# A hybrid decoder block on one core: the heads stage emitted in another order

## The chip, the core and the metric

The kernel runs on one core of a Trainium2 chip. The core has a matrix engine (TensorE, PE in the rows; its weight loads are PEld), three other compute engines (VectorE = DVE, ScalarE = ACT, GpSimd = POOL) and a queue that issues most of its transfers (SyncE = SP). Each engine works through its own list of instructions in the order in which the program was scheduled, and waits where an instruction's inputs or its output buffer are not ready. The metric is the time of one execution on the device in microseconds (us), the median of several runs.

## The reference

One decoder layer over 512 positions of width 1024, in float32. Cut to what matters here:

```
h = rms_norm(x) * (1 + scale1) + shift1            # the conditioning gives six vectors
xr, gr, q, k, v, gm = split(h @ w_in)              # gm: gates of two branches, 2 x 1024
xr = causal_conv4(xr)
r, i = sigmoid(xr @ w_a + b_a), sigmoid(xr @ w_x + b_x)
a = exp(-8 r softplus(-lam));  u = sqrt(1 - a^2) * (i * xr)
hs[t] = a[t] * hs[t-1] + u[t]                      # the recurrence, an associative scan
y_rnn = hs * gelu(gr)
q, k = rope(rms_norm(q) * gq), rope(rms_norm(k) * gk)     # 8 heads, two maps each, 64 wide
o = (softmax(q1 k1^T) - lam softmax(q2 k2^T)) v           # causal, then a norm per head
merged = sigmoid(gm0) * (y_rnn @ w_proj_rnn) + sigmoid(gm1) * (o @ w_proj_attn)
x = x + gate1 * (merged @ w_out)
x = x + gate2 * (relu(h2 @ w_ff1)^2 @ w_ff2)       # h2: norm and modulation again
```

## The kernel before, in words

Every tile has 128 rows; a feature block is 128 features by 512 positions. Products in full precision are made of three matmuls each (`mm3`, lines 129 to 131): every operand is split into a high part (fp32r) and a low part, and high x high, high x low and low x high are added in one PSUM bank. A weight block comes by a transfer (`load_w`), its high part is a cast on ScalarE (wh, line 122), its low part a subtraction on VectorE (wl, line 123), both with two buffers only and at a raised priority; `project` runs 24 matmuls of 512 columns with it.

The stages in order: norm and modulation; projections of the recurrent branch; the first quarter of q and k (heads 0 and 1); convolution, gates of the recurrence and the first half of v; the heads stage; the attention projections (pa) and the merge; the output product; the MLP.

In the heads stage two streams are put together. `heads()` makes the attention heads one after the other, each in four steps i of 128 queries (`softmax_step`: scores sc on TensorE, mask and maximum in one VectorE instruction on line 587, exponential on ScalarE, the weighted difference of the two maps on VectorE line 596; then `weights_t`: transposes aT, their copy aTs; `value_step`: products po; after step 3 `head_norm`). The output of a head is transposed (yT) and split into yah and yal by `head_out`, two steps into the next head (`OUT_AT = 2`). Its buffers: two PSUM banks for the scores (tag sc), one for all transposes (tag tp), one for po (tag o), and four (tag mm) for all the products of the filler.

`fill()` makes the filler, in the order of the string `PLAN` (line 36): g0 to g7 the gates of the first branch (gate functions on line 685), s0 to s7 the recurrence of block n (`lru_scan`: an exponential, line 461, the scan on line 462; `y_rnn`: line 471, then the split into yh and yl), q1 to q3 a quarter of q and k each (heads 2n and 2n + 1), t1 to t3 their transposes and the copies into the form that the heads read, v1 the second half of v, p0 to p7 the projections of the recurrence (each reads all eight yh and yl), m0 to m7 the gates of the second branch (thg). A group between two slashes is emitted at once; after each part of a head step, `UNITS[head] / STEPS` groups are due.

The emitted order is a priority, not the final order: a scheduler lists each engine's instructions by readiness and priority, and a tile whose buffers are all in use waits until an older one is released. The tags that matter: "y" has 24 buffers (`B_Y`, line 69) for the recurrence's inputs, gel, yh and yl, the heads' yah and yal, and thg; wh and wl have two each.

```
yh = slot("y", B_Y, f"yah{hd}", F32R)                 # head_out, line 643
yl = slot("y", B_Y, f"yal{hd}", F32R)
th1.append(gate(KC + n, slot("y", B_Y, f"thg{KC + n}")))    # fill, letter m
```

Of the kernel before, what the change touches and what calls it, by code (L numbers as in the profile page):

```python
# [32 lines left out]

PLAN = ("g0/s0 s1/g1 g2/g3 s2/s3/q1 s4 g4 t1/s5 g5/s6 q2 s7 v1 g6/t2 p0/g7/p1 p2/p3/q3 p4/p5/p6/t3/"
        "p7/m0/m1 m2/m3/m4/m5/m6 m7")
UNITS = [4.25, 5.25, 6.0, 6.75, 5.75, 5.25, 1.75, 5.5]
STEPS = 14
OUT_AT = 2  # L40
# [13 lines left out]
def build(tc, out, x, xT_in, c, pos, vecs, reps, ada, w_xr, w_xr7, w_qk, w_v, w_gr, w_gm, w_lru,  # L54
# [4 lines left out]
    with ExitStack() as es:  # L59
# [636 lines left out]
        def fill():  # L696

            rot = {}
            for group in PLAN.split("/"):
                for op in group.split():  # L700
# [437 lines left out]
```

## Time and profile before

| | us |
|---|---|
| median of 3 runs | 877.34 (877.32 to 877.82) |
| the profiled execution | 876.41 |
| its span, first to last instruction | 874.6 |
| TensorE busy (share of the span) | 861.0 (98%) |
| VectorE busy | 651.5 (74%) |
| ScalarE busy | 449.2 (51%) |

The heads stage lies between about 165 and 455 us of the span. A busy matrix engine means only that a matmul is in flight: a matmul of 512 columns is shown for 0.39 us, though the next one starts 0.23 us after it. Rows of views call tiles by the names in the program with the numbers left out (sc, aT, po, yT, gm, pr). Each window row gives the busy time of each engine in that stretch, and the granted clock of TensorE.

### The profile page before, as it was taken

The page shows a single profiled execution, that of the slowest core. Times are in us where ns is not written, and L with a number is a line of the kernel's source. Part 1 is how long each engine was busy: PE and PEld are TensorE (multiplying, and loading weights), DVE is VectorE, ACT ScalarE, POOL GpSimd, SP SyncE. Part 2 cuts the span into 40 slices and gives each one's busy share as a digit, 9 for nine tenths or more (in the row PEclk, how much of TensorE's full clock was granted, in tenths as well). Part 3 has the DMA queues.
Part 4 walks back from the last instruction along what each step waited for, and adds up shares of the span by engine and source line. Part 5 has one row for each costly group of instructions (what it writes and reads, how often), then busy time and mean ns, then how long its engine had stood idle before and what let it go on. Part 6 is the DMA issues. An engine that isn't in the chain of part 4 may idle for free.

```text
span 874.6 us, 11292 instructions
## 1 busy us (share of the span) xinstructions
PE 861.0 (98%) x4012; PEld 705.5 (81%) x4012; DVE 651.5 (74%) x1251; ACT 449.2 (51%) x748; POOL 15.1 (2%) x50
## 2 busy tenths in 40 slices
PE   6999999999999999999999999999999999999998
PEld 3888887877878888888888888888888888888887
DVE  6997995599859855786758556858766885876397
ACT  6673547985536543535623343747545544554461
POOL 1000000000000000000000000000000000002110
PEclk9999999999999999999999999999999999999999
DMA  8979425412255372238336332822641344139572
GB/s 315 370 250 319 152 97 134 136 68 73 87 131 169 99 191 76 93 87 227 110 126 210 132 121 75 273 87 72 193 148 70 128 161 169 49 126 235 120 122 96
DMA packets 64572, 128.92 MB, mean 147 GB/s; under 512 B 6146, under 2 KB 30850, under 8 KB 64516
## 3 DMA queue, kind: packets, MB, share of 16 engines
q1 hardware_dynamic: 59236, 122.97, 43.3%
q0 software_dynamic: 5280, 5.24, 3.9%
q8 instruction: 31, 0.51, 0.2%
q14 instruction: 25, 0.20, 0.1%
HBM read 113.51 MB, written 2.10 MB: 132 GB/s over the span
## 4 chain that ended last, share of the span: by engine, by line
PE 86%; DVE 10%; DMA 1%; issue 1%; ACT 1%; SPq 1%; ACTq 0%; DVEq 0%
PE f L131 6%; PE f L129 6%; PE f L130 6%; PE X L131 3%; PE X L130 3%; PE X L129 3%; PE gm L129 3%; PE gm L130 3%; PE gm L131 3%; DVE wl L123 2%; PE sc L582 2%; PE qk L131 2%; PE qk L129 2%; PE qk L130 2%; PE xr L129 2%; PE pr L129 2%
## 5 line engine op out<-in xcount | busy, mean ns | idle before, releaser
L122 ACT CAST wh<-w 128x1024 fp32r<-128x1024 f32 (+1 forms) x113 | 118.0, 1044 | 214.5 <-issue 48.1
L123 DVE TENSOR_TENSOR wl<-w,wh 128x1024 fp32r<-128x1024 f32 (+1 forms) x113 | 137.0, 1213 | 68.1 <-ACT wh L122 64.5
L131 PE MATMUL f<-h2h,wl 128*128 128x512 f32 x240 | 93.5, 390 | 0.4 <-DVE wl L123 0.4
L130 PE MATMUL f<-h2l,wh 128*128 128x512 f32 x240 | 93.2, 389 | 0.0
L129 PE MATMUL f<-h2h,wh 128*128 128x512 f32 x240 | 92.9, 390 | 0.0
L131 PEld LDWEIGHTS f<-h2h,wl 128*128 128x128 f32 x240 | 45.0, 188 | 10.1 <-DVE wl L123 0.8
L130 PEld LDWEIGHTS f<-h2l,wh 128*128 128x128 f32 x240 | 45.1, 188 | 9.4
L129 PEld LDWEIGHTS f<-h2h,wh 128*128 128x128 f32 x240 | 45.0, 188 | 9.3
L130 PE MATMUL gm<-hl,wh 128*128 128x512 f32 x128 | 51.0, 398 | 0.0
L129 PE MATMUL qk<-wh,hh 128*128 128x512 f32 x128 | 50.7, 396 | 0.0
L129 PE MATMUL gm<-hh,wh 128*128 128x512 f32 x128 | 50.5, 394 | 0.0
L131 PE MATMUL gm<-hh,wl 128*128 128x512 f32 x128 | 50.5, 394 | 0.0
L131 PE MATMUL qk<-wh,hl 128*128 128x512 f32 x128 | 50.4, 394 | 0.0
L130 PE MATMUL qk<-wl,hh 128*128 128x512 f32 x128 | 50.4, 394 | 0.0
L941 DVE TENSOR_TENSOR p_1l<-b,p_1h 128x1024 fp32r<-128x1024 f32 x24 | 29.4, 1223 | 26.3 <-ACT p_1h L940 26.1
L589 ACT ACTIVATE e<-e,nm 128x128 f32<-128x128 f32 (+3 forms) x64 | 35.7, 559 | 24.4 <-DVE nm L587 24.4
L940 ACT CAST p_1h<-b 128x1024 fp32r<-128x1024 f32 x24 | 25.2, 1051 | 31.0 <-PE f L130 22.9
L941 DVE TENSOR_TENSOR p_0l<-b,p_0h 128x1024 fp32r<-128x1024 f32 x24 | 29.3, 1223 | 15.0 <-ACT p_0h L940 13.8
L587 DVE CUSTOM_DVE_ANT_0 e<-sc,mask 128x128 f32<-128x128 f32 (+3 forms) x64 | 30.3, 484 | 9.9 <-PE sc L582 9.9
L940 ACT CAST p_0h<-b 128x1024 fp32r<-128x1024 f32 x24 | 25.3, 1055 | 24.2 <-PE X L131 12.4
L188 DVE CUSTOM_DVE_ANT_0 ada<-ada,cb,bada 128x1024 f32<-128x1024 f32 x16 | 20.5, 1283 | 14.3 <-DMA ada<-in_ada 14.1
L984 DVE TENSOR_TENSOR b<-b,b 128x1024 f32<-128x1024 f32 x24 | 29.1, 1220 | 0.1
(444 smaller groups left out, 2216.9 us busy)
## 6 DMA issues: line engine op xcount, KB each, us to landing
ada<-in_ada SPq DMA_DIRECT2D x64, 256.0 KB, 5.8
w<-in_w_ff SPq DMA_DIRECT2D x32, 512.0 KB, 3.2
b<-in_w_ff SPq DMA_DIRECT2D x30, 512.0 KB, 3.4
w<-in_w_qk SPq DMA_DIRECT2D x16, 512.0 KB, 3.2
w<-in_w_gm SPq DMA_DIRECT2D x16, 512.0 KB, 3.7
ada<-in_ada SPq DMA_DIRECT2D x16, 512.0 KB, 3.3
b_t<-in_w_ff POOLq DMA_DIRECT2D x10, 512.0 KB, 6.5
w<-in_w_gr SPq DMA_DIRECT2D x8, 512.0 KB, 4.0
```

The costliest lines, as they stand in the source:

```text
L122: i_w = nc.scalar.copy(wh[:, :n], w[:, :n])
L123: nc.vector.tensor_tensor(wl[:, :n], w[:, :n], f32(wh)[:, :n], op=ALU.subtract)
L129: nc.tensor.matmul(ps, lh, rh, start=first, stop=False, skip_group_check=more)
L130: nc.tensor.matmul(ps, lh, rl, start=False, stop=False, skip_group_check=more)
L131: nc.tensor.matmul(ps, ll, rh, start=False, stop=last, skip_group_check=more)
L188: nc.vector.tensor_tensor_reduce(w, w, cb, 1.0, bada[:, col:col + 1], op0=ALU.mult, op1=ALU.add, accum_out=mod[:, col:col + 1])
L582: nc.tensor.matmul(ps[m][:, :nn], q[m][:, qc], k[m][r][:, :nn], start=r == 0, stop=r == 1)
L587: nc.vector.tensor_tensor_reduce(e[:, :n], ps[m][:, :n], mask[:, S - n:], 1.0, 1e30, op0=ALU.add, op1=ALU.min, accum_out=nm)
L589: nc.scalar.activation(e[:, :n], e[:, :n], AF.Exp, bias=nm, scale=-1.0, accum_out=sums[:, m:m + 1])
L940: nc.scalar.copy(v4(wh), v)
L941: nc.vector.tensor_tensor(v4(wl), v, f32(v4(wh)), op=ALU.subtract)
L984: nc.vector.tensor_tensor(d, d, s_, op=ALU.add)
```

## The change

Only the string that orders the filler is another one. The recurrences s1 to s7 are spread over more groups, g4 stands ahead of the second quarter and g6 ahead of the third, and m0 ahead of p0; the number of groups grows by one.

```
-PLAN = ("g0/s0 s1/g1 g2/g3 s2/s3/q1 s4 g4 t1/s5 g5/s6 q2 s7 v1 g6/t2 p0/g7/p1 p2/p3/q3 p4/p5/p6/t3/"
-        "p7/m0/m1 m2/m3/m4/m5/m6 m7")
+PLAN = ("g0/s0/g1 g2/s1 g3/g4/q1 t1/s2 g5/s3/g6 s4 q2 s5 v1/s6 t2/g7 s7/m0/p0 p1/p2/q3 p3/p4/p5/t3/"
+        "p6/p7/m1 m2/m3/m4/m5/m6 m7")
```

Three places of the resulting order follow. The number behind a tile's name counts the program's tiles, so a tile has another one after the change.

TensorE before, in the last quarter of q and k (qk_0 to qk_3: its four PSUM banks), 12 rows after the transposes of head 3's output (yT); aT_1_3535 are the transposes of step 1 of head 4:

```order
L129 MATMUL qk_1_3541<-wh_3546,hh_195 128x512
L130 MATMUL qk_1_3541<-wl_3547,hh_195 128x512
L131 MATMUL qk_1_3541<-wh_3546,hl_199 128x512
L129 MATMUL qk_1_3541<-wh_3546,hh_238 128x512
L130 MATMUL qk_1_3541<-wl_3547,hh_238 128x512
L131 MATMUL qk_1_3541<-wh_3546,hl_242 128x512
L604 MATMUL aT_1_3535<-ident,e_1_0_3459 128x128 x2
L129 MATMUL qk_2_3542<-wh_3546,hh_195 128x512
```

TensorE after, at the same transposes (aT_1_3504 now); pr_4272 is the eighth projection of the recurrence (p7), and yh_1831, yh_1959 and yh_2512 are blocks 0, 1 and 2:

```order
L131 MATMUL pr_4272<-yh_1831,wl_4269 128x512
L129 MATMUL pr_4272<-yh_1959,wh_4268 128x512
L130 MATMUL pr_4272<-yl_1961,wh_4268 128x512
L131 MATMUL pr_4272<-yh_1959,wl_4269 128x512
L129 MATMUL pr_4272<-yh_2512,wh_4268 128x512
L130 MATMUL pr_4272<-yl_2514,wh_4268 128x512
L604 MATMUL aT_1_3504<-ident,e_1_0_3396 128x128 x2
L131 MATMUL pr_4272<-yh_2512,wl_4269 128x512
L129 MATMUL pr_4272<-yh_2577,wh_4268 128x512
L130 MATMUL pr_4272<-yl_2579,wh_4268 128x512
L615 MATMUL po_3387<-vs_0_3159,aTs_1_3507 128x128
```

Step 1's transposes of head 4 have moved from the first unit of the last quarter into the last projection of the recurrence: 220 filler rows now stand between them and head 3's yT.

TensorE before, around step 2 of head 6 (sc_2_0 and sc_2_1 the scores of its two maps, aT_0 and po_4145 the transposes and products of step 0, gm_4424 the gate product m2):

```order
L129 MATMUL gm_4424<-hh_346,wh_4420 128x512
L130 MATMUL gm_4424<-hl_350,wh_4420 128x512
L131 MATMUL gm_4424<-hh_346,wl_4421 128x512
L582 MATMUL sc_2_0_4203<-kh_2_0_4038,qs_0_0_4023 128x384
L604 MATMUL aT_0_4197<-ident,e_0_0_4134 128x128
L582 MATMUL sc_2_0_4203<-kl_2_0_4041,qs_0_0_4023 128x384
L582 MATMUL sc_2_1_4204<-kh_2_1_4044,qs_0_1_4026 128x384
L582 MATMUL sc_2_1_4204<-kl_2_1_4047,qs_0_1_4026 128x384
L615 MATMUL po_4145<-vs_0_3133,aTs_0_4199 128x128
L129 MATMUL gm_4424<-hh_398,wh_4420 128x512
L130 MATMUL gm_4424<-hl_402,wh_4420 128x512
L131 MATMUL gm_4424<-hh_398,wl_4421 128x512
```

TensorE after, at the same step (po_4146 its products, yT_4222 the transposes of head 5's output, gm_4588 the gate product m5):

```order
L582 MATMUL sc_2_0_4204<-kh_2_0_4078,qs_0_0_4063 128x384
L582 MATMUL sc_2_0_4204<-kl_2_0_4081,qs_0_0_4063 128x384
L604 MATMUL aT_0_4198<-ident,e_0_0_4135 128x128
L582 MATMUL sc_2_1_4205<-kh_2_1_4084,qs_0_1_4066 128x384
L582 MATMUL sc_2_1_4205<-kl_2_1_4087,qs_0_1_4066 128x384
L615 MATMUL po_4146<-vs_0_3159,aTs_0_4200 128x128
L642 MATMUL yT_4222<-ident,o_4019 128x128 x4
L582 MATMUL sc_3_0_4239<-kh_2_0_4078,qs_0_0_4063 128x512
L582 MATMUL sc_3_0_4239<-kl_2_0_4081,qs_0_0_4063 128x512
L582 MATMUL sc_3_1_4240<-kh_2_1_4084,qs_0_1_4066 128x512
L582 MATMUL sc_3_1_4240<-kl_2_1_4087,qs_0_1_4066 128x512
L129 MATMUL gm_4588<-hh_195,wh_4584 128x512
```

The gate rows that stood between the scores of steps 1, 2 and 3 are gone from there: they ran ahead of them (gm_4530) or come behind (gm_4588).

VectorE before, at the start of head 6 (e_0_0 and e_0_1: mask and maximum of the two maps of step 0; ql_3: the low part of the last transposed quarter, wl_4459: the weight split of m3):

```order
L123 TENSOR_TENSOR wl_4421<-w_4418,wh_4420 128x1024
L587 ISA e_0_0_4134,nm_0_0_4133<-sc_0_0_4127,mask 128x128
L587 ISA nm_0_0_4133 128x1
L143 TENSOR_TENSOR ql_3_4072<-qT_3_4065,qh_3_4070 128x512
L587 ISA e_0_1_4138,nm_0_1_4137<-sc_0_1_4128,mask 128x128
L587 ISA nm_0_1_4137 128x1
L123 TENSOR_TENSOR wl_4459<-w_4456,wh_4458 128x1024
```

VectorE after, at the same start (wl_4585 and wl_4632: the weight splits of m5 and m6):

```order
L123 TENSOR_TENSOR wl_4585<-w_4582,wh_4584 128x1024
L587 ISA e_0_0_4135,nm_0_0_4134<-sc_0_0_4128,mask 128x128
L587 ISA nm_0_0_4134 128x1
L143 TENSOR_TENSOR ql_1_4097<-qT_1_4090,qh_1_4095 128x512
L123 TENSOR_TENSOR wl_4632<-w_4629,wh_4631 128x1024
L587 ISA e_0_1_4139,nm_0_1_4138<-sc_0_1_4129,mask 128x128
L587 ISA nm_0_1_4138 128x1
L593 RECIPROCAL rr_4126<-sm_0_4127 128x2
```

The split wl_4632 has moved in between the two maps of step 0; its cast reuses the buffer that the product gm_4530 reads.

## Rows read from the trace of the kernel before

**Rows 1.** The page: engine totals, and slices of TensorE's busy share and clock.

```profile
PE 861.0 (98%) x4012; PEld 705.5 (81%) x4012; DVE 651.5 (74%) x1251; ACT 449.2 (51%) x748; POOL 15.1 (2%) x50
...
PE   6999999999999999999999999999999999999998
...
PEclk9999999999999999999999999999999999999999
```

**Rows 2.** Windows: stretch, its length, busy us of each engine, clock, transfers.

```profile
178.00:218.00 40.00, 38.15 (x194) 30.58 (x194) 39.86 (x98) 26.86 (x64) 0.00 (x0) 1.00 0.19 66
...
190.00:200.00 10.00, 8.90 (x53) 7.10 (x52) 9.91 (x25) 6.77 (x19) 0.00 (x0) 1.00 0.21 76
...
240.00:250.00 10.00, 9.26 (x43) 7.08 (x42) 8.83 (x22) 2.59 (x3) 0.00 (x0) 1.00 0.27 96
...
380.00:447.00 67.00, 66.96 (x356) 54.64 (x355) 47.60 (x149) 34.65 (x92) 0.00 (x0) 1.00 0.52 153
...
419.00:437.00 18.00, 17.96 (x101) 14.59 (x101) 13.94 (x49) 10.99 (x32) 0.00 (x0) 1.00 0.25 88
```

**Rows 3.** Waits, heads stage: who waited for whom, total us, times, longest.

```profile
PE aT L604 <- DVE e L596: 1.5, 4, 0.7
PE qT L547 <- DVE raw L535: 0.7, 1, 0.7
...
ACT wh L122 <- PE gm L130: 15.0, 10, 3.9
```

**Rows 4.** The tile yT from 355 to 395 us: durations (ns), first and last start.

```profile
L642 PE MATMUL yT<-ident,o x4: 270/272/273, 366.4 to 366.8; 128*128 128x128 f32 x4
L644 ACT ACTIVATE yah<-yT,sg x1: 678/678/678, 379.6 to 379.6; 128x512 fp32r<-128x512 f32 x1
L646 DVE SCALAR_TENSOR_TENSOR yal<-yT,sg,yah x1: 743/743/743, 380.7 to 380.7; 128x512 fp32r<-128x512 f32 x1
```

**Rows 5.** The tile thg on ScalarE, 395 to 450 us.

```profile
L685 ACT ACTIVATE thg<-gm x8: 589/592/631, 411.4 to 447.9; 128x512 f32<-128x512 f32 x8
```

**Rows 6.** Timeline from 418 to 428 us: start, duration, engine, line, tiles, idle before.

```profile
418.83 0.29 DVE L587 CUSTOM_DVE_ANT_0 e<-sc,mask 128x128 f32<-128x128 f32 x1
...
419.84 0.28 PE L582 MATMUL sc<-kh,qs 128*128 128x256 f32 x1
419.93 0.17 DVE L593 RECIPROCAL rr<-sm 128x2 f32<-128x2 f32 x1 [0.80 <-ACT e L589]
419.95 0.28 PE L582 MATMUL sc<-kl,qs 128*128 128x256 f32 x1
...
421.55 0.34 PE L582 MATMUL sc<-kh,qs 128*128 128x384 f32 x1
...
421.72 0.34 PE L582 MATMUL sc<-kl,qs 128*128 128x384 f32 x1
...
424.44 0.55 DVE L587 CUSTOM_DVE_ANT_0 e<-sc,mask 128x384 f32<-128x384 f32 x1
...
425.87 1.05 ACT L122 CAST wh<-w 128x1024 fp32r<-128x1024 f32 x1
...
426.13 0.60 PE L642 MATMUL yT<-ident,o 128*128 128x128 f32 x4
...
426.48 0.48 PE L582 MATMUL sc<-kl,qs 128*128 128x512 f32 x1
...
426.80 0.39 PE L582 MATMUL sc<-kh,qs 128*128 128x512 f32 x1
...
426.95 1.23 DVE L123 TENSOR_TENSOR wl<-w,wh 128x1024 fp32r<-128x1024 f32 x1
427.03 0.40 PE L582 MATMUL sc<-kl,qs 128*128 128x512 f32 x1
```

**Rows 7.** Groups by line, VectorE, 165 to 455 us: the scans and their neighbours.

```profile
L462 DVE TENSOR_TENSOR_SCAN xc<-r,xc 128x512 f32<-128x512 f32 x8 | 9.7, 1210 | 0.0
```

## The prediction

> **What bounds the kernel now.** I read the page first: TensorE is busy for 98% of the span, at a clock of 1.00 in every slice (2.4 GHz), so a changed order can only win or lose time in which TensorE stands [rows 1]. Then the windows of the heads stage. From 178 to 218 us TensorE is busy 38.15 of 40 us and VectorE 39.86: here VectorE's queue decides, and TensorE loses 1.85 us. From 380 to 447 us, the last heads, TensorE is busy 66.96 of 67 us and VectorE 47.60: nothing is lost there, because a matmul of the filler stands ready behind every step of a head [rows 2]. A third place loses 0.74 us (240 to 250). The waits by name agree: transposes of weights that wait for VectorE's weighted sum (1.5 us), and one wait of the second quarter's transposes (0.7 us) [rows 3]. So at most 2.6 us are to be won in this stage, while the end of it has 19 us of idle VectorE time and no TensorE time to spare.
>
> Two more views show what holds the heads. The four transposes that end head 4 ran from 366.4 us, but their copies on ScalarE and VectorE only at 379.6 and 380.7 [rows 4]. In between the last recurrence projections ran. The copies go into buffers of tag "y", 24 of them; the eight recurrence results take 16 until the last projection reads them, and the outputs of heads 0 to 3 take the other 8. The next transposes of this head need the same single PSUM buffer, so the heads stood for 13 us, and TensorE lived on filler. And the first second-branch gate (thg) left its PSUM bank only at 411.4 us, though four banks are all that the filler products have [rows 5].
>
> **The change, part by part.** No instruction is added but a few splits of merged waits; the work is the same, in another order.
>
> *The hold comes a head earlier.* The first second-branch gate (m0) now stands before the first projection, so one "y" buffer more is taken: 16 + 1 + 6 = 23 when head 3 ends, one is left, and head 3's low part finds none. By the order on TensorE the held transposes (aT of step 1, head 4) come after 8 rows of the eighth projection, 220 filler rows after the transposes of head 3; before, the hold (head 5) was 60 rows long. A row starts 0.23 us after the one before it (426.80 and 427.03) [rows 6], so 60 rows are 13.7 us, which is what rows 4 show, and the new hold is about 50 us. While it lasts nothing is lost: TensorE has its 220 rows. What is lost comes behind it: the rest of head 4 and heads 5, 6 and 7 must run beside 16 + 168 rows, where before the rest of head 5 and heads 6 and 7 had 12 + 192 rows. The tail gets one head more and one gate product less.
>
> *Term A, a wait in front of head 6.* The four PSUM banks are full (gates 1 to 4) when gate 4's product ends, since the gate function of gate 1 now stands on ScalarE behind an exponential of head 6, step 2. So the next filler can't start. In VectorE's queue a weight split (wl_4632) stands ahead of the mask-and-max of the second map of step 0, and it waits for a cast that waits for the last row of gate 4's product, whose buffer it takes; such casts waited 15 us in all for gate products before, where filler covered it [rows 3]. From that last row's start: 0.39 us for the row, 1.08 from cast to split, 1.14 for the split to the next start (1.23 less the 0.08 by which a next one starts early), 0.29 for the mask-and-max: 2.90 us until TensorE may write the bank again [rows 6]. It has in the meantime the row itself (0.23), four 256-wide score rows (0.12 each) and four transposes (0.35 to the next start at 426.48, so 0.09 each; I take 0.44 with the hand-over): 1.1 us. A = 2.9 - 1.1 = **1.8 us**. Bounds: 0 if the bank is freed by another path, 2.0 with a delay of 0.1 at each hand-over.
>
> *Term B, the chain of head 6.* Behind it TensorE's queue has only rows of this head up to the last score of step 3, and each waits for VectorE. The same chain in head 7 before, from the mask-and-max of step 0 (418.83) to the end of that of step 2 (424.44 + 0.55), took 6.2 us, with a wait of 0.80 us for an exponential in it [rows 6]; TensorE filled it with gate rows. There it also held eleven tiny instructions of the norm, which are elsewhere now (up to 1.8 us, some in gaps), and now holds one 512-wide split (0.69). I take 5.3 us, less the first 0.29: 5.0. TensorE's work in it: scores of 0.24 + 0.35 + 0.35 + 0.46 (256-wide 0.12 a row, 384-wide 0.17, 512-wide 0.23), a transpose and a value row of 0.11, and four transposes of 0.44, together 2.06. B = 5.0 - 2.1 = **2.9 us**; bounds 2.3 (one more overlap) and 3.8 (the whole measured 6.2).
>
> *Term C, the rest of the tail.* One head more costs VectorE no more than 11.4 us (13.94 busy from 419 to 437, which holds all of head 7, less one split of 1.23 and one 1.29), so it goes from 47.6 to at most 57.9 of 67 us with one split of 1.14 gone [rows 2]. That still fits, so throughput asks for nothing; but the steps of heads 4, 5 and 7 now have 2 to 10 rows between them. Nearest rows: this tail before lost 0.04, and the stretch where VectorE was full lost 1.85 in 40 us, which over 67 us is 3.1. I take **2.0**, bounds 0 and 4.
>
> *Term D, the front.* In VectorE's order the scans are hardly later: a scan is 1.21 us [rows 7], and the eighth now comes before step 2 of head 1 is summed, where it came after step 3. What changes is that one gate product more (24 rows, 5.5 us of TensorE) stands before the second quarter, with its split (1.14), and three of the splits of finished recurrences (0.60 each) slip behind the stretch: VectorE 39.86 - 0.7 = 39.2 us against TensorE's 38.15 + 5.5 = 43.6. The queue is no longer full, but two scans in a row now stand ahead of a sum that a transpose waits for. I take **-1.0**, bounds 0 and -1.85. The 0.74 us at 245 stays: its chain and the 92 rows that cover it are the same; its bounds are 0 and -0.74.
>
> The SP queue issues the same transfers; the weight loads of gates 4 to 6 pass the copies of the last quarter, and a load has two products' time (11 us) to land, so nothing is charged.
>
> The sum: 1.8 + 2.9 + 2.0 - 1.0 = +5.7 us. The profiled execution took 876.41 us (span 874.6), so it would take 882.1; the median shown is 0.93 above that execution, which gives **883.0 us**.
>
> One rule of the Trainium skill speaks against this. "Perfetto Trace Analysis", Optimization Strategy, says that where the most-contended engine changes over time, interleaving the regimes can help. Rows 2 show such regimes (VectorE 39.86 of 40 us in one, 47.60 of 67 in the other), and by the rule alone the sum would be term D with the 0.74, at most -2.6 us: the first rival below.
>
> **The rivals.**
> 1. *The front's waits go and the tail keeps its cover* (faster). The scans spread out, TensorE gets the 1.85 us and some of the 0.74 back, and A and B vanish because the gate functions free their banks in time. For it: TensorE was full in the tail (0.04 lost), and VectorE has 19 us there. Against: 57.9 of 67 us and the order itself, which puts no filler row between the scores of head 6. About -2: 875.3 us.
> 2. *The front's gain pays for a small tail* (no change): only B's lower end counts and D is full: 2.3 - 1.85 = +0.5: 877.8 us.
> 3. *The order does not do what it says*: the scans stay where they were, D is 0, and the tail costs what I sum: +6.7, 884.0 us. It lies inside my own range.
> 4. *VectorE becomes the bound of the whole tail* (worse): waits for exponentials of 0.80 us at two or three places of each step add up to C = 4 to 6 on top of A and B at their upper bounds (5.8): +10, 887.4 us. It decides if VectorE's busy share from the release to the last head's norm is above 9 tenths.
> 5. *The clock falls.* Before, a window with 1.10 us of idle TensorE kept 1.00 [rows 2]; no row shows a longer gap after the start. If the half-filled 7 us of A and B brought the granted clock to its lower level (1.2 GHz), one gate product behind it would take twice its 5.5 us: +11.2, 888.5 us. The Trainium skill, "TensorE: Matmul & The Clock Gate", HAM oscillation, states that idle gaps can throttle the array again; the rows so far (1.00 in every window) don't bear that out here.
>
> **How the numbers follow.** My forecast (+3 to +9, with rival 3) has 0.74, rival 4 0.08, rival 5 0.03, rival 2 0.07, rival 1 0.08. About 0.2% (1.75 us) is what a measurement can tell from no change: slower 0.86 (mine, 4, 5 and 0.01 of rival 2), same 0.06, faster 0.08. With all low bounds (A 0, B 2.3, C 0, D -1.85 and -0.74) the sum is -0.3, with all high ones +9.8, and rivals 4 and 5 go on to +11; I leave out a tenth at either end: 878.6 to 888.0 us.
>
> **What would show it.** Right: the copies of head 3's output 45 us or more after its transposes; TensorE full while they wait; then, in the last 70 us before the attention projections, a stretch of some 7 us with about 4.7 us of idle TensorE, in which the waits are named after mask-and-max and the sums; the first second-branch gate but one leaving its bank only there; and 178 to 223 us with about 1 us less idle time. Wrong: gate rows running between the scores of head 6; or the loss lying in front of 230 us; or no wait longer than 1 us in the tail.

## The result, and the profile after

The changed kernel takes 884.24 us (median of 5 runs, 883.65 to 884.72), the kernel before 877.34 us in the same comparison (876.54 to 877.91): a ratio of 1.0077 with a 95% interval of 1.0063 to 1.0092. That is slower, as forecast (883.0 us, range 878.6 to 888.0). The profiled execution took 883.81 us with a span of 882.0, 7.4 us more than before.

The page of the changed kernel, its engine totals and the granted clock:

```profile
PE 864.7 (98%) x4012; PEld 707.4 (80%) x4012; DVE 652.4 (74%) x1251; ACT 449.6 (51%) x748; POOL 15.1 (2%) x50
...
PEclk9999999999999999999899999999999999999999
```

TensorE runs the same 4012 instructions, but is busy for 3.7 us longer than in [rows 1] and idle for 3.7 us longer (17.3 against 13.6 us). So half of the loss is idle time, and the other half is rows that are shown for longer; one slice of the clock row has an 8 instead of a 9. The windows of the changed kernel say where (columns as in [rows 2]):

```profile
178.00:218.00 40.00, 37.83 (x191) 30.79 (x190) 39.44 (x93) 25.35 (x60) 0.00 (x0) 1.00 0.19 66
...
250.00:290.00 40.00, 39.27 (x205) 32.14 (x205) 30.20 (x86) 21.99 (x54) 0.00 (x0) 1.00 0.59 158
...
410.00:420.00 10.00, 8.61 (x43) 6.68 (x41) 5.18 (x11) 3.61 (x6) 0.00 (x0) 1.00 0.85 217
420.00:430.00 10.00, 8.91 (x35) 6.67 (x36) 6.90 (x26) 6.35 (x18) 0.00 (x0) 0.66 0.79 213
```

The front did not get better: 2.17 us idle from 178 to 218 us against 1.85 in [rows 2], and the 0.73 us of the second quarter's chain are there again, 5 us later. The tail lost 2.48 us of idle time in 20 us, and a third of the clock in the second half of them; VectorE was busy for only 12 of those 20 us.

Idle time does not see rows that are merely slower or further apart. So this table measures losses otherwise: from the start of each matmul to the start of the next one, less the median of that difference for its width (0.227 us for 512 columns, 0.177 for 384, 0.119 for 256, 0.109 for 128, from the kernel before). The sum over a stretch is what TensorE lost there, in us:

| stretch, us | before | changed | e1 | e2 | e3 | e5 | e9 |
|---|---|---|---|---|---|---|---|
| 178 to 230 | 3.7 | 3.6 | 3.6 | 3.7 | 3.5 | 3.5 | 3.8 |
| 230 to 375 | 2.9 | 2.6 | 2.9 | 2.9 | 2.8 | 2.7 | 3.1 |
| 375 to 410 | 0.9 | 1.9 | 1.1 | 1.2 | 1.2 | 1.9 | 1.1 |
| 410 to 432 | 0.9 | 6.8 | 0.8 | 8.7 | 1.1 | 0.7 | 0.9 |
| 432 to 470 | 0.3 | 1.4 | 0.7 | 3.0 | 1.2 | 6.1 | 0.3 |

Changed less before, before rounding, gives -0.1, -0.3, +1.0, +6.0 and +1.1: 7.6 us. Ahead of 178 us the changed kernel lost 0.4 us less, which leaves 7.3 of the 7.4 us.

Now the tile yT of the changed kernel from 300 to 470 us, which answers to [rows 4]:

```profile
L644 ACT ACTIVATE yah<-yT,sg x5: 670/688/690, 329.3 to 460.1; 128x512 fp32r<-128x512 f32 x5
L646 DVE SCALAR_TENSOR_TENSOR yal<-yT,sg,yah x5: 745/750/751, 378.7 to 460.8; 128x512 fp32r<-128x512 f32 x5
```

The first of the five is head 3's output. Its high part was copied at 329.3, its low part 49.4 us later: the one buffer of tag y that was left went to the high part, and the low part waited until the last recurrence projection gave buffers back. Before, the hold was 13 us and a head later. While the low part waited, TensorE was full, with 222 rows:

```profile
329.00:379.00 50.00, 50.00 (x222) 41.16 (x220) 27.70 (x49) 15.87 (x21) 0.00 (x0) 1.00 0.30 100
```

ScalarE's copies of outputs (L644) and second-branch gate functions (L685), changed kernel (start, duration, idle before):

```profile
329.34 0.67 ACT L644 ACTIVATE yah<-yT,sg 128x512 fp32r<-128x512 f32 x1
...
424.97 0.69 ACT L644 ACTIVATE yah<-yT,sg 128x512 fp32r<-128x512 f32 x1 [1.74 <-PE yT L642]
...
426.15 0.58 ACT L685 ACTIVATE thg<-gm 128x512 f32<-128x512 f32 x1
...
427.23 0.59 ACT L685 ACTIVATE thg<-gm 128x512 f32<-128x512 f32 x1
...
428.46 0.60 ACT L685 ACTIVATE thg<-gm 128x512 f32<-128x512 f32 x1
```

Between 329 and 426 us no gate function of the second branch runs; those of m1, m2 and m3 then come one after the other, the first 1.2 us behind the copy of head 5's output. Their products had ended at 396.0, 405.2 and 411.1 us, that of m4 at 417.5; until then m1 to m4 fill all four PSUM banks. TensorE in the same place:

```profile
418.26 0.36 PE L582 MATMUL sc<-kl,qs 128*128 128x256 f32 x1
420.11 0.39 PE L582 MATMUL sc<-kh,qs 128*128 128x256 f32 x1 [1.49 <-DVE nm L587]
420.34 0.28 PE L582 MATMUL sc<-kl,qs 128*128 128x256 f32 x1
421.44 0.69 PE L582 MATMUL sc<-kh,qs 128*128 128x384 f32 x1 [0.82 <-DVE nm L587]
421.93 0.52 PE L582 MATMUL sc<-kl,qs 128*128 128x384 f32 x1
...
425.58 0.63 PE L582 MATMUL sc<-kh,qs 128*128 128x512 f32 x1
426.01 0.63 PE L582 MATMUL sc<-kl,qs 128*128 128x512 f32 x1
426.79 0.79 PE L129 MATMUL gm<-hh,wh 128*128 128x512 f32 x1 [0.15 <-ACT thg L685]
```

Two waits for mask-and-max, and then slower rows: they are shown for 0.52 us with 384 columns and 0.63 with 512, where [rows 6] have 0.34 and 0.40, and two of 512 start 0.43 us apart (425.58 and 426.01) instead of 0.23. The first gate row after them waits for the first gate function. VectorE shows what the first wait is:

```profile
418.62 1.23 DVE L123 TENSOR_TENSOR wl<-w,wh 128x1024 fp32r<-128x1024 f32 x1 [0.83 <-PE sc L582]
419.77 0.28 DVE L587 CUSTOM_DVE_ANT_0 e<-sc,mask 128x128 f32<-128x128 f32 x1
```

That is the weight split which now stands between the two maps of step 0. The view names another releaser, but it starts right behind the cast that it reads (417.56 to 418.59 us). And the clock, in windows of 2 us of the changed kernel:

```profile
418.00:420.00 2.00, 0.62 (x5) 0.42 (x4) 1.38 (x3) 1.13 (x2) 0.00 (x0) 1.00 0.64 137
420.00:422.00 2.00, 1.06 (x4) 0.80 (x4) 1.40 (x8) 1.08 (x4) 0.00 (x0) 0.72 0.71 152
422.00:424.00 2.00, 2.00 (x8) 1.53 (x7) 1.59 (x7) 0.62 (x3) 0.00 (x0) 0.50 0.40 89
424.00:426.00 2.00, 2.00 (x8) 1.72 (x7) 1.34 (x6) 1.03 (x2) 0.00 (x0) 0.50 0.96 207
426.00:428.00 2.00, 1.85 (x7) 0.95 (x6) 1.04 (x4) 1.81 (x6) 0.00 (x0) 0.57 0.90 237
```

### The profile page after: what moved, and what is told of

Read it like the earlier page. It is cut to its first block, busy times and chain, and to the rows that moved or that the text cites. A ratio compares the mean times of both kernels' runs of the same rounds, so it can differ in the third digit from the quotient of the medians.

```text
span 882.0 us, 11295 instructions
## 1 busy us (share of the span) xinstructions
PE 864.7 (98%) x4012; PEld 707.4 (80%) x4012; DVE 652.4 (74%) x1251; ACT 449.6 (51%) x748; POOL 15.1 (2%) x50
## 4 chain that ended last, share of the span: by engine, by line
PE 89%; DVE 7%; ACT 1%; issue 1%; DMA 1%; SPq 0%; ACTq 0%
PE f L131 6%; PE f L130 6%; PE f L129 6%; PE X L130 3%; PE X L131 3%; PE X L129 3%; PE gm L129 3%; PE gm L130 3%; PE gm L131 3%; PE qk L131 3%; PE qk L130 3%; PE qk L129 3%; PE sc L582 2%; PE po L615 2%; PE xr L129 2%; PE v L129 2%
## 5 line engine op out<-in xcount | busy, mean ns | idle before, releaser
L129 PEld LDWEIGHTS gm<-hh,wh 128*128 128x128 f32 x128 | 24.2, 189 | 5.0 <-ACT thg L685 0.9
```

The lines of the kernel that those rows point to most:

```text
L129: nc.tensor.matmul(ps, lh, rh, start=first, stop=False, skip_group_check=more)
```

## The experiments

Twelve kernels ran, each against the kernel before on the same chip in five rounds (its medians there were 876.8 to 877.1 us). Five settle the cause, two the clock, five the front. e1 stands for the label e1_m0_behind, and so on.

**Is it m0's place?** Back behind p7 in the changed order:

```
-g7 s7/m0/p0 p1/p2/q3 p3/p4/p5/t3/p6/p7/m1 m2/
+g7 s7/p0 p1/p2/q3 p3/p4/p5/t3/p6/p7/m0/m1 m2/
```

> The changed order with one letter moved back: m0 behind p7 instead of ahead of p0. Theory 1 (the buffer that m0's gate takes starts the hold a head earlier, and all of the loss lies in the tail behind it): head 4 runs on as before, the hold falls on head 5, the stretch around head 6 loses under 1.5 us instead of 6.8, and the time is 876.5 to 878.0 us (+0.0 +-0.1% against the kernel before). Theory 2 (the loss comes from the other moves, the scans and the gates ahead of the second and third quarter): m0's place does not matter, 883 to 885 us.

Measured: 877.3 us, ratio 1.0005 (0.9996 to 1.0013). And m0 moved ahead of p0 in the order before (the group of t2 and p0 is split for it, so the string has one group more, as the changed one has):

```
-g6/t2 p0/g7/  ...  p7/m0/m1 m2/
+g6/t2/m0/p0/g7/  ...  p7/m1 m2/
```

> The order before with one letter moved: m0 ahead of p0 instead of behind p7. Theory 1: this alone makes the hold of some 50 us on head 4 and the idle time and the lower clock in head 6; 883 to 885 us (+0.7 +-0.15%). Theory 2: 877 to 878 us.

Measured: 887.78 us, ratio 1.0125 (1.0109 to 1.0140). The same window of both, e1 first and then e2:

```profile
420.00:430.00 10.00, 9.84 (x53) 8.02 (x52) 8.24 (x35) 7.17 (x24) 0.00 (x0) 1.00 0.16 54
```

```profile
420.00:430.00 10.00, 8.93 (x29) 6.48 (x29) 6.03 (x24) 5.24 (x15) 0.00 (x0) 0.53 0.76 175
```

One letter makes all of the loss, whichever order it stands in; the scans and the other gates make none, nor does the number of groups, which e1 leaves as the change has it. e2 is 2.8 us above the expected upper end: its last head waits too (3.0 us from 432 to 470).

**Its place, or its buffer?** The changed order, with m0's output elsewhere:

```
-slot("y", B_Y, f"thg{KC + n}")
+slot(*(("y", B_Y) if n else ("v", B_V)), f"thg{KC + n}")
```

> The changed order word for word, but the output of m0's gate goes into a buffer of the value tiles (tag v, free when head 3 is done) instead of tag y. Theory 1: 16 + 8 outputs fit again, the hold moves back to head 5, 877 to 879 us, with a first gate function of the second branch that still comes behind head 5's output. Theory 2, and also the rival that it is m0's place in the row of products and not its buffer: 883 to 885 us.

Measured: 878.24 us, ratio 1.0014 (1.0006 to 1.0023). The next one leaves m0 in tag y and gives the outputs of heads 3 and 4 the four value buffers, so that no head waits:

```
+where = ("v", B_V) if hd in (3, 4) else ("y", B_Y)
-yh = slot("y", B_Y, f"yah{hd}", F32R)            # yal alike
+yh = slot(*where, f"yah{hd}", F32R)
```

> The changed order word for word; the outputs of heads 3 and 4 go into the four value buffers that are free after head 3, so that no head waits for tag y (m0 stays ahead of p0 and in tag y). If the hold and nothing else makes the loss: no copy of an output waits longer than 3 us for a buffer, the tail loses under 1.5 us, 876.5 to 878.5 us. If the hold is only half of it (m0 used up ahead of time is missing as filler at the end): 879 to 882 us, with the loss behind 440 us.

Measured: 877.33 us, ratio 1.0002 (0.9994 to 1.0011). So it is the buffer. With the order of the instructions' source unchanged, one or four buffers more take back 6 to 7 us, and m0 run early is not missed as filler at the end.

**Is it the four banks?** The gate functions of m1 to m4 in the value buffers, the hold left as it is:

```
-slot("y", B_Y, f"thg{KC + n}")
+slot(*(("v", B_V) if 1 <= n <= 4 else ("y", B_Y)), f"thg{KC + n}")
```

> The changed order word for word; the outputs of the gates m1 to m4 go into the four value buffers that are free after head 3 instead of tag y. The hold on head 4 stays as it is (50 us). Theory 1a (tag y hands out its buffers in the program's order, so the gate functions of m1 to m4 wait for head 5's output to take its own, and the four PSUM banks they sit in starve TensorE of filler): the gate functions run 1 to 3 us behind their products, gate rows stand between the scores of head 6, the stretch from the release to the end of head 6 loses under 2 us instead of 6.8, 878.5 to 880.5 us. Theory 1b (the squeezed heads are bound by VectorE's chain whatever the banks do): TensorE still waits 2 us or more for mask-and-max in head 6, 882 to 885 us.

Measured: 882.54 us, ratio 1.0064 (1.0051 to 1.0077). The time lies in the range of 1b, while head 6 does what 1a expected. ScalarE in e5:

```profile
395.79 0.69 ACT L644 ACTIVATE yah<-yT,sg 128x512 fp32r<-128x512 f32 x1 [1.14 <-PE yT L642]
...
397.31 0.60 ACT L685 ACTIVATE thg<-gm 128x512 f32<-128x512 f32 x1
...
407.94 0.58 ACT L685 ACTIVATE thg<-gm 128x512 f32<-128x512 f32 x1
...
412.26 0.59 ACT L685 ACTIVATE thg<-gm 128x512 f32<-128x512 f32 x1
```

The gate functions no longer wait for head 5's output (424.9 us): they run 0.8 to 2.3 us behind their products, against 17 to 30 in the changed kernel. Head 6 loses nothing (0.7 us from 410 to 432). That much of 1a is right: what they waited for is their turn in tag y. In the five kernels where they share it with the heads' outputs (before, changed, e1, e2, e3), the first of those left at that point starts 0.6 to 1.9 us behind the copy of head 5's output, whenever that comes, from 411 to 427 us. But the gate rows that cover head 6 are then missing behind head 7. TensorE in e5:

```profile
459.20 0.63 PE L642 MATMUL yT<-ident,o 128*128 128x128 f32 x4 [1.26 <-DVE o L635]
460.61 1.21 PE L129 MATMUL pa<-yah,wh 128*128 128x512 f32 x2 [0.78 <-ACT yah L644]
```

The stretch from 432 to 470 us lost 6.1 us instead of 1.4. The banks decide where the tail starves, not whether: three and a half heads are left for too little filler.

**What does the lower clock cost?** Useless matmuls into the two gaps of head 6, kept there by order (`after`); their products go into the bank of head 6's value products:

```
+for _ in range(DUMMY[i, m, r]):
+    d_ = nc.tensor.matmul(pre[0], ident, ct..., start=True, stop=True)
+    after(d_, mms[-1])
```

> The changed order with nine useless matmuls of 512 columns in the two gaps of head 6 (six in front of the second map's scores of step 1, three in front of those of step 2; they write a bank that is overwritten). The waits for mask-and-max stay; TensorE is only busy in them. Theory C (the two gaps, 1.5 and 0.8 us, bring the clock down, and the lower clock is some 3 us of the loss): the granted clock stays 1.00 from 418 to 430 us and the time falls to 880 to 882 us. Rival (the clock falls for another reason, or its rows lie beside waits that stay anyway): no change, 883.5 to 885 us.

Measured: 890.39 us, ratio 1.0153 (1.0139 to 1.0167). This run says nothing on the clock: a plain float32 product of 512 columns shows as two rows, 0.43 us from start to start, so nine of them took 7.7 us and outlasted the gaps, and the second three also overwrote a value product (that part of the output is lost) and were waited for. The next kernel uses fp32r operands, and both sets come before any value product:

```
-nc.tensor.matmul(pre[0], ident, ct..., start=True, stop=True)
+nc.tensor.matmul(pre[0], h[0][0][:, :P], h[0][0], start=True, stop=True)
```

> The changed order, every instruction in its place, with nine useless matmuls of 0.23 us in the two gaps of head 6 (six behind the second map's scores of step 0, three behind those of step 1; they write a bank that is overwritten). The fillers of e6_gap_filled took 0.86 us each, so they outlasted the gaps; these do not. Theory C (the two gaps bring the clock down, and the lower clock is some 3 us of the loss): the granted clock stays 1.00 from 418 to 430 us, the stretch from 410 to 432 us loses 3 to 4.5 us instead of 6.8 besides the 2.1 us of useless rows that lie in waits, 880 to 882 us. Rival (the lower clock costs nothing on the path, since head 6 waits for VectorE anyway): 883.5 to 885 us, with waits for mask-and-max longer by what the rows are shorter.

Measured: 883.2 us, ratio 1.0071 (1.0058 to 1.0083), between the two expected ranges. Two windows of e10 that answer to the third and fourth of the 2 us rows above:

```profile
422.00:424.00 2.00, 1.72 (x10) 1.26 (x10) 1.58 (x9) 1.11 (x3) 0.00 (x0) 1.00 0.64 138
424.00:426.00 2.00, 1.86 (x8) 0.87 (x8) 1.32 (x5) 2.00 (x7) 0.00 (x0) 1.00 0.96 206
```

The clock stays up when the gaps are filled, so the gaps brought it down. But faster rows only wait longer: idle time now stands where slow rows stood. The stretch from 410 to 432 us lost 3.6 us and spent 2.0 on the useless rows, 5.6 together, against 6.8. That makes 1.2 us for the clock in the profiles, not 3. The intervals of the two ratios overlap, so the times alone do not show it. One reason lies at the end of the program: the last matmul of e10 starts 2.0 us earlier than that of the changed kernel (876.60 against 878.56 us; 0.4 of it was won ahead of 178 us), but from there to the end of the span e10 takes 4.9 us and the changed kernel 3.4. Why its end is longer stays open.

**Why did the front win nothing?** In the next kernels each recurrence's first VectorE step stands behind the last weighted sum ahead of it in the program. In e7 that is all that changes from the kernel before:

```
+if last_sum:
+    after(i_, last_sum[-1])
```

> The order before, but each recurrence's first VectorE step may not start before the last weighted sum that stands ahead of it in the program, so that the scans stand where the order's string has them: 3, 1, 1, 3 and so on per step instead of up to 7 ahead of a step. Theory D (the 1.85 us of idle TensorE from 178 to 218 us come from scans that VectorE runs ahead of sums): 1 to 1.9 us won, 875.0 to 876.5 us, and VectorE no longer 99% busy there. Rival (VectorE's work in this stretch is the same whatever its order, and the waits only change places): 876.5 to 878.5 us.

Measured: 877.47 us, ratio 1.0005 (0.9996 to 1.0014). The same in e8, on top of e1:

> The changed order with m0 back behind p7 and with the scans pinned to their places in the string, which are spread out to heads 1 to 3. Theory D: the front's waits go (1.85 us and more), the tail is as before: 874.5 to 876.5 us, faster than both kernels. Rival: the waits change places, 876.5 to 879 us.

Measured: 883.06 us, ratio 1.0074 (1.0061 to 1.0087). Windows of e8, the front and the stretch behind it:

```profile
178.00:218.00 40.00, 40.00 (x203) 33.50 (x202) 29.48 (x78) 24.47 (x59) 0.00 (x0) 1.00 0.23 79
...
262.00:340.00 78.00, 73.84 (x362) 58.51 (x361) 70.45 (x189) 41.66 (x100) 0.00 (x0) 0.98 0.47 132
```

Theory D is right about the front: with the scans really spread out, VectorE falls to 29.48 us and TensorE does not wait at all there. By starts, 178 to 230 us lost 0.6 instead of 3.7 us. But now six scans run from 268 to 318 us, beside the norm of the third quarter and in front of the projections that need them, and 230 to 375 us lost 11.5, so the time is above both expected ranges. Two orders between the extremes (e11: s2, s3 ahead of q1; e13: s4 to s7 behind q1):

```
-g4/q1 t1/s2 g5/s3/g6 s4 q2 s5 v1/s6 t2/g7 s7/
+s2/g4/s3 q1 s4 t1/g5/s5 g6/s6 q2 s7 v1/t2/g7/          # e11
+s2/g4/s3 q1 s4 s5 s6 s7 t1/g5/g6/q2 v1/t2/g7/          # e13
```

> The changed order with m0 back behind p7 and the scans pinned, but s2 to s7 each put a group or two earlier than in e8_m0_behind_scans_pinned (s2 and s3 before the second quarter, s7 before the second half of v), so that the last one ends before 290 us. Theory D (VectorE's full queue costs the front its 1.85 us, and in e8 only the projections that waited for the last yh lost 8 us): the front loses 1 to 2 us instead of 3.6, the projections do not wait, 874.8 to 876.5 us. Rival (each scan that is moved costs as much beside the later heads): 876.5 to 878.5 us.

Measured: 877.77 us, ratio 1.0007 (0.9998 to 1.0016).

> As e11_scans_spread (m0 behind p7, scans pinned), but the last three recurrences stand behind the second quarter's products (s5 to s7 between q1 and t1) instead of beside heads 2 and 3: in e11 VectorE was busy for 12 of 24 us from 214 to 226 and from 256 to 268 us, and for 24 of 24 from 268 to 286 and 292 to 298 us. Theory D (what counts is that VectorE is full nowhere while a head runs): the front keeps its 2.5 us, the stretch from 262 to 375 us loses under 2 us instead of 4.9, 874.5 to 876.0 us, ratio under 0.9985. Rival (the three recurrences now delay the norm of the second quarter, for which TensorE waits at 245 us): 876.5 to 878.5 us.

Measured: 879.05 us, ratio 1.0027 (1.0018 to 1.0036), above both expected ranges. In the traces both win 2.5 us in the front (1.2 lost instead of 3.7) and give them back: e11 loses 4.9 us from 262 to 375 (before: 1.6), e13 loses 3.8 from 230 to 262 (before: 1.3), most of it in one wait for the norm of the second quarter:

```profile
251.80 0.30 PE L549 MATMUL qT<-ident,raw 128*128 128x128 f32 x1 [2.67 <-DVE raw L537]
```

The profiled execution of e13 was the fastest of its eleven (877.10 us), so the trace does not show all of its loss: in six others the mean granted clock was 0.998 instead of 1.000, and these took 878.75 to 880.50 us against 877.10 to 879.05. No trace shows where the clock fell in them.

The rival holds in all four: between 178 and 375 us, moving scans moved the waits, and in e8 and e13 made them dearer. The last kernel takes work away from VectorE instead, on the kernel before:

```
-nc.vector.tensor_tensor(hs, hs, g, op=ALU.mult)
+nc.gpsimd.tensor_tensor(hs, hs, g, op=ALU.mult)
```

> The kernel before with the eight products of scan and gelu (0.68 us each on VectorE) on GpSimd, which stands idle in this stretch. If VectorE's busy share of 99% from 178 to 218 us is what makes TensorE wait there, 5.5 us less on VectorE win 0.5 to 1.8 us: 875.2 to 876.6 us. Rival (GpSimd is so slow that the splits behind it come late, or it takes time from VectorE): 877 to 880 us.

Measured: 886.5 us, ratio 1.0106 (1.0093 to 1.0119), far above both expected ranges. The product's row in e12:

```profile
L471 POOL TENSOR_TENSOR xc<-xc,gel x8: 1262/1632/2117, 181.5 to 215.3; 128x512 f32<-128x512 f32 x8
```

1.63 us instead of 0.68, in a chain that TensorE waits for: 178 to 230 us lost 13.5 us. No kernel tried beats the kernel before; e1, e7, e9 and e11 equal it.

## Why the prediction was right, point by point

- **The hold** (220 rows, about 50 us, a head earlier, by m0's buffer): 49.4 us between the two parts of head 3's output, and e2, e3 and e9 show that this buffer is the cause.
- **Terms A and B** (1.8 + 2.9 = 4.7 us around head 6): the stretch lost 6.0 us more than before. The run with the clock held up (e10) lost 3.6 + 2.0 - 0.9 = 4.7 more, so the chain was sized right. The wait of A was 1.49 us (1.7 from start to start); the first of B was 0.82. Of the 4.7 us of idle time that the prediction gave as a sign, 2.48 show as idle; the rest shows as slower rows. What the sum left out is the clock, 1.2 us by the profiles. It was a rival by itself (chance 0.03, 888.5 us), with its price taken for a whole gate product behind the gap. It fell on rows of a chain that waits for VectorE anyway, so it cost less than the 3 us that e10 was expected to show.
- **The reason given in A for the full banks** was half right. The gate function of m1 does stand behind an exponential of step 2, but what put it there is the turn of head 5's output in tag y. e5 shows it, and shows too that freeing the banks moves 4.7 us to the last head.
- **Term C** (2.0 us, bounds 0 and 4): 375 to 410 and 432 to 470 us lost 1.0 + 1.1 = 2.1 more. The figure was taken between two far rows (0.04 and 3.1), so that it fits so closely is luck in part.
- **Term D** (-1.0 us) is the step that failed. The queue was forecast at 39.2 of 40 us and called "no longer full"; it was 39.44, and TensorE waited as long as before. One wait took the place of most of the waits for sums in [rows 3]: head 0's output transposes, behind its norm. TensorE and VectorE of the changed kernel, and the last scan of the kernel before:

```profile
209.45 0.66 PE L642 MATMUL yT<-ident,o 128*128 128x128 f32 x4 [1.70 <-DVE o L635]
```

```profile
195.95 2.33 DVE L462 TENSOR_TENSOR_SCAN xc<-r,xc 128x512 f32<-128x512 f32 x2
...
212.74 1.20 DVE L462 TENSOR_TENSOR_SCAN xc<-r,xc 128x512 f32<-128x512 f32 x1
```

```profile
220.08 1.22 DVE L462 TENSOR_TENSOR_SCAN xc<-r,xc 128x512 f32<-128x512 f32 x1
```

The string puts the scans later and further apart; the finished order puts the last one 7 us earlier, and two in a row. A string of priorities does not hold back what is ready, as e7 and e8 show, where a dependency does. By starts the front won 0.1 us, so D was 0.9 too good. With that, the 1.2 of the clock, the 0.1 of C and the 0.3 won from 230 to 375 us, the forecast sum of 5.7 becomes 7.6 us, and with the 0.4 won ahead of 178 us 7.2, against 7.4 in the spans (6.9 in the medians).
- **The second quarter's 0.74 us** stayed (0.73).
- **The rivals**: the first (faster) and the second (no change) needed the tail to keep its cover; it did not. The third, D at 0, is what happened in the front. The fourth needed VectorE above 9 tenths from the release to the last norm:

```profile
379.00:459.00 80.00, 77.18 (x401) 62.10 (x400) 57.51 (x186) 42.24 (x118) 0.00 (x0) 0.96 0.44 132
```

57.51 of 80 us is 7 tenths. The tail is bound by a chain that crosses engines with nothing beside it, not by an engine's total.

## What to carry to other kernels

Before moving a product ahead of others, count what its result holds until it is read, in the pool it shares: here one more live buffer of 24 cost 7 us, 100 us further on, through a head that could not put its output away. m0 itself was not missed as filler (e9); what cost time was that the held heads came behind filler that had run while they stood. When filler runs short like this, freeing the banks only chooses where the engine starves (e5). And an order given as priorities is not an order until the instruction lists, or the trace, show it.

## What the hardware showed that was not expected

In the profiled execution of e13 a single gap of 2.67 us left TensorE's granted clock at 1.00 (the row above; its windows follow), and in the changed kernel one of 1.70 us did (209 us).

```profile
250.00:252.00 2.00, 0.20 (x2) 0.23 (x3) 1.83 (x7) 0.00 (x0) 0.00 (x0) 1.00 0.86 221
252.00:254.00 2.00, 2.00 (x12) 1.43 (x12) 1.46 (x3) 1.01 (x1) 0.00 (x0) 1.00 0.10 41
```

Two gaps of 1.49 and 0.82 us with two short score rows between them brought it to 0.50, that is 1.2 GHz; so did 1.26 and 0.78 us around four transposes in e5, whose 512-column rows then show 0.63 us. In these traces the longest gap alone does not tell. Nor does one execution: six of the eleven of e13 had a lower mean clock (0.998) without a trace to say where, so the row does not show that a gap of 2.67 us is always harmless.

The Trainium skill, "TensorE: Matmul & The Clock Gate", HAM oscillation, describes this by gaps in which TensorE waits. The runs agree that such gaps can bring the clock down (changed kernel, e5), and e10 that filling them keeps it up.

A tensor product on GpSimd took 1.63 us for 128x512 where VectorE needs 0.68, and while GpSimd worked, VectorE's L461 of the same shape went from 679 to 821 ns on average (e12, 178 to 218 us).
